# A scheduled trunk of sparse attention, short convolution and SwiGLU: when memory counts as free in the order, and new durations for small operations

## The chip, the core and the metric

The kernel runs on one core of a Trainium2 chip. The core has a matrix engine (PE, whose weight loads are shown apart as PEld), a vector engine (DVE), a scalar engine (ACT), GpSimd (POOL) and the sync engine (SP), from which nearly all DMAs of this kernel are issued. Each engine works off its own queue in order. The metric is the time of one execution on the device in microseconds.

## What is computed

Two decoder layers on 1024 tokens of width 1024, in float32. The first layer mixes tokens by sparse attention: an indexer scores all earlier keys, the best 256 of each query are kept, and attention runs over those. The second mixes by a gated convolution of width 3. Each is followed by a SwiGLU FFN of width 2816, and shift, scale and gate of every norm come from a conditioning vector.

```python
def reference(x, c, positions, ada_w, ada_b, ...):
    c_act = jax.nn.silu(c)
    for i in range(DEPTH):
        mod = c_act @ ada_w[i] + ada_b[i]
        sh1, sc1, g1, sh2, sc2, g2 = [m[:, None, :] for m in jnp.split(mod, 6, axis=-1)]
        h = _rmsnorm(x, norm1_g[i]) * (1.0 + sc1) + sh1
        if i % N_MIXERS == 0:
            y = _dsa_mixer(h, positions, ...)
        else:
            y = _short_conv_mixer(h, ...)
        x = x + g1 * y
        h = _rmsnorm(x, norm2_g[i]) * (1.0 + sc2) + sh2
        x = x + g2 * _swiglu(h, ffn_w_gate[i], ffn_w_up[i], ffn_w_down[i])
    return x
```

## The kernel before

The program is written in two steps. The classes `Attention` and `Tail` record operations with the tiles that they read and write; `Plan` then puts them in order, at build time, and emits them engine by engine. On the chip nothing is decided any more: each engine runs its queue as emitted and waits on semaphores where data or memory aren't ready.

`Plan.drain` is a list scheduler. It holds for each engine the time at which it is free (`self.free`), takes from each engine the recorded operation that could start first, breaks ties by a priority (`pri`, then the order of recording), and places the earliest of all. How long an operation takes is told by `Plan.cost`, in microseconds, from its engine, its name and its free size; `LATENCY` and `SLACK` are added between engines, and a DMA ends after a fixed 1.6 and its bytes at a set rate. A copy recorded by `Plan.copy` may go to ACT or to DVE, whichever is free earlier by these figures. So a price in `cost` never makes anything faster or slower by itself. It only moves operations in the queues.

Memory is handled in pools (`Pool`). Each pool has a gate: no tile of it is given out, in the plan, before `gate.ready`. When a pool is opened (`Plan.open`) this is set to the smallest free time of all engines. What the chip does is apart from that: a pool that lies where another lay waits on the real last use of the tiles there (`reuse_waits="tile"`).

The order of pools stands at the end of `trunk_kernel`. The projections and the selection use `h` and `pj`; attention uses `kp` (the keys, tile `karena`), `at` (rows of the softmax and other small things), the PSUM pool `pa` (banks `ps_L` and `ps_o`), and on the right side `keep`, `sel` and `op` (the attention's output, `ohi` and `olo`). When all operations of `kp`, `at` and `pa` are placed, the pools of the tail are opened in their place: the PSUM pool `pg`, and `x2` (the residual, tile `xr`), `u` and `h2` as `f.first`. When `keep`, `sel` and `op` are done, `t2` and `s2` follow as `f.second`.

Around the first of these changes the following is recorded, all with one priority and so in this sequence: `Attention.attended` makes the eight output tiles of the second half (`out_tile`: a weight load of 512 KB into `raw`, two splits of it into a high and a low half, `whi` on ACT and `wlo` on DVE, 48 matmuls, and an addition into `xr`). After the first of them it starts the tail's first norm of the other half (`norm_first`): eight squares on ACT from `xr` to `u`, sums on DVE, a transposition on PE into `ps_g`, a root, and the operands `h`. A raw tile has two buffers and the split halves four each, so the splits of the third tile wait for matmuls of the first. The sixteen loads of `xr` (`xr<-xs` in the trace) come from DRAM, the half for the output tiles and the half for the norm.

From there on the products of the FFN and the convolution run (`Pair` and `down_pairs`, a Strassen form with seven products for eight), with side steps of the conditioning between them (`adaw` loads, `adacc` on DVE).

All instructions carry line 272, that of the helper that emits them, so the profile is read by tile names.

Of the kernel before, what the change touches and what calls it, by code (L numbers as in the profile page):

```python
# [14 lines left out]
AF = mybir.ActivationFunctionType  # L15
ALU = mybir.AluOpType
AX = mybir.AxisListType
PSUM = bass.MemoryType.PSUM
# [32 lines left out]
class Store:  # L51


    def __init__(self, space):
        self.space, self.real, self.parts = space, None, {}
        self.alloc = None
        self.ring, self.late, self.begun, self.todo, self.last = None, False, False, 0, 0.0
# [49 lines left out]
class Op:  # L107
# [3 lines left out]
    def __init__(self, eng, cost, emit, pri, lat=0.0):  # L111
        self.eng, self.cost, self.emit, self.pri, self.lat = eng, cost, emit, pri, lat
        self.left, self.ready, self.users, self.end, self.stores = 0, 0.0, [], None, ()
        self.late, self.other, self.form = 0.0, None, None
        self.needs, self.parked = [], False


class Pool:


    def __init__(self, plan, name, side=None, space=None, bufs=1, **rings):
        self.depth = rings
        self.plan, self.name, self.side, self.space, self.bufs = plan, name, side, space, bufs
        self.gate = Op(None, 0.0, lambda: None, 0)
        self.gate.left = 1
        self.rings, self.pending = {}, 0

    class Ring:
        def __init__(self, plan, bufs):
# [56 lines left out]
class Plan:  # L186
# [48 lines left out]
    def cost(self, eng, fn, out, ins, kw):  # L235

        n = out.free
        if fn == "dma_start":
            if eng == "gpsimd":
                return 0.85, 1.6  # L240
            inside = len(ins) == 1 and all(r.store.alloc is not None for r in ins + [out])
            return {"sync": 0.65 if inside else 0.475, "scalar": 0.1}[eng], 1.6
        if eng == "tensor":
            if fn == "transpose":
                return 0.107, 0.0
            if ins[1].dtype in (F32R, BF16):
                return max(n, 64) * 17 / 38400.0, 0.0
            return max(n * 4, 512) / (4800.0 if HD in (ins[0].free, ins[0].shape[0]) else
                                      2400.0), 0.0
        psum = any(r.store.space == PSUM for r in ins + [out])  # L250
        m = max([n] + [r.free for r in ins])
        aps = sum(r.free == 1 for r in ins)
        if eng == "scalar":
            return 0.03 + 0.95e-3 * n + (0.09 if "accum_out" in kw else 0.0) + 0.1 * aps, 0.0
        if eng == "vector":
            if fn == "memset":
                return 0.02 + 1.04e-3 * (n if n > P else 0), 0.0
            if fn in ("tensor_scalar", "tensor_copy") and not psum and "accum_out" not in kw:
                return (0.08 if fn == "tensor_copy" else 0.13) + 0.52e-3 * m, 0.0
            if fn == "tensor_scalar" and "accum_out" in kw:  # L260
                return 0.14 + 1.04e-3 * m, 0.0
            return 0.07 + 1.04e-3 * m + (0.05 * aps if m > 64 else 0.0), 0.0
        if fn in ("memset", "affine_select"):
            return 0.05 + 1.4e-3 * n, 0.0
        a, w = (0.28, 1.95e-3) if fn == "tensor_tensor" else (0.43, 1.3e-3)
        return a + w * (n - 1), 0.0
# [34 lines left out]
    def record(self, eng, fn, args, kw, other=None):  # L301
        vals = list(args) + list(kw.values())
        outs = [kw["out"] if "out" in kw else args[0]]
        if "accum_out" in kw:
            outs.append(kw["accum_out"])
        refs = [v for v in vals if isinstance(v, Ref)]
        ins = [v for v in refs if not any(v is o for o in outs)]
        emit = self.emitter(eng, fn, args, kw)
        shaped = outs[0] if isinstance(outs[0], Ref) else refs[0]
        cost, lat = self.cost(eng, fn, shaped, ins, kw)  # L310
        self.count += 1
        pri = (self.count if self.pri is None else self.pri, self.count)
        op = Op(eng, cost, emit, pri, lat)
        if "accum_out" in kw:
            op.late = 0.13 if eng == "vector" else 0.1
        if other is not None:
            op.other = (other[0], self.cost(*other[:2], shaped, ins, kw)[0],
                        self.emitter(*other, args, kw))
        if fn == "dma_start":
            op.lat = lat + shaped.free * shaped.shape[0] * 4 / 380e3  # L320
        self.note(op, refs, outs)
        return op
# [58 lines left out]
            u.ready = max(u.ready, self.after(op, u))  # L381
            self.settle(u)

    def open(self, pool, stack):
        kw = {}
        if pool.space is not None:
            kw["space"] = pool.space
        if pool.side is not None:
            kw["side"] = pool.side
        pool.handle = stack.enter_context(  # L390
            self.tc.tile_pool(name=pool.name, bufs=pool.bufs, reuse_waits="tile", **kw))
        pool.gate.left = 0
        pool.gate.ready = min(self.free.values())
        self.settle(pool.gate)
        return pool

# [84 lines left out]
    def drain(self, *pools):  # L481

        held = []
        while any(p.pending for p in pools) if pools else True:
            best, again = None, False
            for e in self.ENGINES:
                got = self.next(e)
                if got is None:
                    continue
                op = got[3][-1]  # L490
                if op.other is not None and e != op.eng and self.sooner(op, got[0]):
                    held.append((e, op))
                    self.drop(*got[2:])
                    again = True
                    break
                if best is None or got[0] < best[0]:
                    best = got
            if again:
                continue
            for e, op in held:  # L500
                if op.end is None:
                    at = max(op.ready, best[0] if best else 0.0)
                    heapq.heappush(self.soon[e], (at, op.pri, op))
            held = []
            if best is None:
                assert not any(p.pending for p in pools), \
                    "nothing can be issued: " + str([(p.name, p.pending) for p in pools])
                return
            t, e, heap, v = best
            op = v[-1]  # L510
            self.drop(heap, v)
            self.place(op, t)
            if e != op.eng:
                op.eng, op.cost, op.emit = op.other
            op.emit()
            cost = op.cost
            if e == "tensor":
                cost = cost * self.clock(t, cost) + self.CHANGE.get((self.form, op.form), 0.0)
                self.form = op.form
            self.free[e] = end = t + cost  # L520
            if op.lat:
                self.dma = max(self.dma, end) + (op.lat - 1.6)
                end = self.dma + 1.6 + (op.lat - 1.6) * 380e3 * self.TRAIL
                if e == "sync":
                    self.free[e] = max(self.free[e], self.dma - 2.5)
            for st in op.stores:
                if st.alloc is not None:
                    st.pool.pending -= 1
            self.finish(op, end)
            for st in op.stores:  # L530
                st.todo -= 1
                st.last = max(st.last, end if op.lat else end + 0.25)
                if st.todo == 0 and st.ring is not None:
                    st.ring.back(st.last)

# [305 lines left out]
def trunk_kernel(tc, x, c, positions, ada_w, ada_b, norm1_g, norm2_g, attn_w_in, attn_q_norm_g,  # L841
                 attn_k_norm_g, idx_k_ln_g, idx_k_ln_b, attn_w_out, conv_w_in, conv_w,
                 conv_w_out, ffn_w_gate, ffn_w_up, ffn_w_down, rope_c, out):
    plan = Plan(tc.nc, tc)
    with ExitStack() as ctx:
        ctx.enter_context(tc.manual_schedule())
        tk = Trunk(plan)
# [4 lines left out]
        a = Attention(tk, attn_w_in[0], attn_w_out[0], ada_w, xspill)  # L852
# [5 lines left out]
        f = Tail(tk, ada_w, xspill)  # L858
        a.attended(f)
        f.run(ffn_w_gate, ffn_w_up, ffn_w_down, conv_w_in[0], conv_w_out[0], out)  # L860
        right, proj, left = (ctx.enter_context(ExitStack()) for _ in range(3))
# [8 lines left out]
        plan.drain(a.kp, a.at, tk.pa)  # L870
        left.close()
        for p in (tk.pg, *f.first):
            plan.open(p, left)
        plan.drain(a.keep, a.sel, a.op)
        right.close()
        for p in f.second:
            plan.open(p, left)
        plan.drain()


# [1094 lines left out]
```

## Time and profile before

| | us |
|---|---|
| median of 3 runs | 2287.06 (2284.31 to 2287.76) |
| the profiled execution, its time | 2284.62 |
| its span, first to last instruction | 2282.7 |
| PE busy | 2204.1 |
| DVE busy | 1908.3 |
| ACT busy | 1136.6 |

The difference of 1.9 us between time and span lies around the instructions. The mean granted clock of PE was 0.983 of full. Durations of neighbouring instructions on one engine overlap in the profile: the pace is read from the starts of instructions that follow one another, or from a row of several, less one duration. The text tells times from the start of the span; a name such as `whi<-raw` gives the tile written and the tile read.

### The profile page before, as it was taken

How to read it: one execution, taken by the hardware profiler on the slowest of the kernel's cores; microseconds unless marked ns; L12 is line 12 of the kernel's file. 1: busy time of each engine (PE TensorE's matmuls, PEld its weight loads, DVE VectorE, ACT ScalarE, POOL GpSimd, SP SyncE). 2: the span in 40 equal slices, each digit the busy share in tenths (PEclk: the TensorE clock that was granted, in tenths of full speed). 3: DMA queues.
4: the chain of work that ended last, by engine and by line, in shares of the span. 5: the costliest groups of instructions: out<-in, count | busy, mean ns of one | idle time of the engine just before them, and what ended most of it. 6: DMA issues, size and time to landing. Idle time of an engine off the chain costs nothing.

```text
span 2282.7 us, 32575 instructions
## 1 busy us (share of the span) xinstructions
PE 2204.1 (97%) x11435; PEld 1781.5 (78%) x11435; DVE 1908.3 (84%) x3839; ACT 1136.6 (50%) x2152; POOL 4.8 (0%) x19
## 2 busy tenths in 40 slices
PE   4999989999999999999999999999999999999999
PEld 3757866876798878888888778788888888888887
DVE  7899998898589998887788999786898877767974
ACT  4587889857655323333445552224453333334444
POOL 0000000000000000000000000000000000000000
PEclk7999989999999999999999999999999999999999
DMA  9313333542244665544982354424446432339824
GB/s 321 108 47 87 97 104 89 163 147 91 97 140 139 216 215 169 160 147 151 379 306 101 103 165 139 125 79 157 120 125 194 152 120 88 125 128 387 291 89 138
DMA packets 332317, 353.72 MB, mean 155 GB/s; under 512 B 19289, under 2 KB 216954, under 8 KB 332154
## 3 DMA queue, kind: packets, MB, share of 16 engines
q1 hardware_dynamic: 331944, 351.52, 47.6%
q8 instruction: 89, 1.46, 0.3%
q14 instruction: 74, 0.61, 0.1%
q10 hardware_dynamic: 210, 0.14, 0.0%
HBM read 278.97 MB, written 68.94 MB: 152 GB/s over the span
## 4 chain that ended last, share of the span: by engine, by line
PE 71%; DVE 15%; DMA 4%; ACT 2%; issue 2%; SPq 0%; ACTq 0%; DVEq 0%
PE ps_g L272 41%; PE ps_mm L272 28%; DVE u L272 2%; DVE wlo L272 2%; DVE s L272 2%; PE ps_o L272 2%; PE ps_L L272 1%; DVE sc L272 1%; DVE adacc L272 1%; DVE v L272 1%; DMA adaw<-in_ada_w_dram 1%; DVE karena L272 1%; DVE p L272 1%; ACT p L272 1%; DVE cv L272 1%
## 5 line engine op out<-in xcount | busy, mean ns | idle before, releaser
L272 ACT CAST whi<-raw 128x512 fp32r<-128x512 f32 (+1 forms) x312 | 191.8, 619 | 381.0 <-PE ps_g L272 165.9
L272 PE MATMUL ps_g<-t,whi 128*128 128x512 f32 x1184 | 368.8, 393 | 2.4 <-ACT whi L272 2.3
L272 ACT CAST whi<-s 128x512 fp32r<-128x512 f32 x276 | 171.3, 621 | 328.8 <-PE ps_g L272 140.9
L272 PE MATMUL ps_g<-h,whi 128*128 128x512 f32 x1056 | 326.0, 390 | 0.0
L272 DVE TENSOR_TENSOR wlo<-raw,whi 128x512 fp32r<-128x512 f32 (+1 forms) x314 | 214.5, 684 | 76.5 <-ACT whi L272 76.2
L272 PEld LDWEIGHTS ps_g<-t,whi 128*128 128x128 f32 x1184 | 223.7, 190 | 50.8 <-ACT whi L272 4.6
L272 PE MATMUL ps_g<-t,wlo 128*128 128x512 f32 x592 | 233.2, 395 | 4.8 <-DVE wlo L272 4.6
L272 PEld LDWEIGHTS ps_g<-h,whi 128*128 128x128 f32 x1056 | 197.7, 188 | 40.8
L272 PE MATMUL ps_g<-h,wlo 128*128 128x512 f32 x528 | 205.8, 390 | 2.1 <-DVE wlo L272 2.0
L272 DVE TENSOR_TENSOR wlo<-s,whi 128x512 fp32r<-128x512 f32 x276 | 188.0, 684 | 20.9 <-ACT whi L272 19.8
L272 PE MATMUL ps_mm<-t,whi 128*128 128x512 f32 x608 | 188.1, 390 | 0.2
L272 PE MATMUL ps_g<-ph,whi 128*128 128x512 f32 x572 | 179.3, 389 | 0.0
L272 PEld LDWEIGHTS ps_g<-t,wlo 128*128 128x128 f32 x592 | 112.5, 190 | 30.9 <-DVE wlo L272 7.4
L272 PEld LDWEIGHTS ps_mm<-t,whi 128*128 128x128 f32 x608 | 114.4, 188 | 25.2 <-ACT whi L272 0.9
L272 PEld LDWEIGHTS ps_g<-ph,whi 128*128 128x128 f32 x572 | 107.4, 188 | 22.2
L272 DVE TENSOR_TENSOR u<-u 128x512 f32<-128x512 f32 x170 | 114.2, 684 | 7.4 <-ACT u L272 6.2
L272 ACT ACTIVATE junk<-sc,bs 128x896 bf16<-128x896 f32 (+3 forms) x124 | 109.7, 884 | 18.7 <-DVE bs L272 8.7
L272 PE MATMUL ps_mm<-t,wlo 128*128 128x512 f32 x304 | 118.7, 391 | 0.0
L272 PEld LDWEIGHTS ps_g<-h,wlo 128*128 128x128 f32 x528 | 99.1, 188 | 23.5 <-DVE wlo L272 3.0
L272 DVE SCALAR_TENSOR_TENSOR adacc<-adaw,cact,adacc 128x512 f32<-128x512 f32 x140 | 104.2, 745 | 12.6 <-DMA adaw<-in_ada_w_dram 12.2
L272 PE MATMUL ps_g<-ph,wlo 128*128 128x512 f32 x286 | 110.9, 389 | 0.0
L272 PE MATMUL ps_mm<-hhi,whi 128*128 128x512 f32 (+2 forms) x240 | 93.7, 391 | 6.0 <-ACT hhi L272 3.3
(311 smaller groups left out, 4775.2 us busy)
## 6 DMA issues: line engine op xcount, KB each, us to landing
adaw<-in_ada_w_dram SPq DMA_DIRECT2D x160, 256.0 KB, 2.9
ph<-in_ffn_w_down_dram SPq DMA_DIRECT2D x66, 512.0 KB, 6.5
raw<-in_ffn_w_gate_dram SPq DMA_DIRECT2D x54, 512.0 KB, 4.2
raw<-in_ffn_w_up_dram SPq DMA_DIRECT2D x54, 512.0 KB, 4.1
raw<-in_conv_w_in_dram SPq DMA_DIRECT2D x34, 512.0 KB, 4.2
raw<-in_ffn_w_down_dram SPq DMA_DIRECT2D x44, 256.0 KB, 2.7
ph<-in_ffn_w_down_dram SPq DMA_DIRECT2D x44, 256.0 KB, 5.0
raw<-in_attn_w_in_dram SPq DMA_DIRECT2D x18, 512.0 KB, 3.9
```

The lines of the kernel that those rows point to most:

```text
L272: f(*[a.get() if isinstance(a, Ref) else a for a in args], **{k: a.get() if isinstance(a, Ref) else a for k, a in kw.items()})
```

## The change

It has two parts. In the first, a pool remembers the latest end of an operation that used a tile of it (`Pool.last`), `Plan.open` takes the pools whose memory the new one takes over, and the gate is the latest of the smallest free time and their last uses. `pg` follows `pa`; `x2` follows `kp`; `u` and `h2` follow `at`; `t2` and `s2` follow `keep`, `sel` and `op`. The pools opened earlier are as they were. In the second part, `Plan.cost` has other figures for ACT (by where the source lies, and with a term for two functions), for DVE's `tensor_scalar`, scan and reciprocal, and for the common DVE operation, with a least value of 0.09. No operation is added, dropped or given other operands.

```diff
@@ -123,7 +123,7 @@
         self.plan, self.name, self.side, self.space, self.bufs = plan, name, side, space, bufs
         self.gate = Op(None, 0.0, lambda: None, 0)
         self.gate.left = 1
-        self.rings, self.pending = {}, 0
+        self.rings, self.pending, self.last = {}, 0, 0.0
 
     class Ring:
         def __init__(self, plan, bufs):
@@ -251,15 +251,19 @@
         m = max([n] + [r.free for r in ins])
         aps = sum(r.free == 1 for r in ins)
         if eng == "scalar":
-            return 0.03 + 0.95e-3 * n + (0.09 if "accum_out" in kw else 0.0) + 0.1 * aps, 0.0
+            slow = {AF.Silu: 0.06, AF.Square: 0.03}.get(kw.get("func"), 0.0)
+            return ((0.05 if (ins or [out])[0].store.space == PSUM else 0.095) + 0.84e-3 * n + slow +
+                    (0.09 if "accum_out" in kw else 0.0) + 0.1 * aps), 0.0
         if eng == "vector":
             if fn == "memset":
                 return 0.02 + 1.04e-3 * (n if n > P else 0), 0.0
             if fn in ("tensor_scalar", "tensor_copy") and not psum and "accum_out" not in kw:
-                return (0.08 if fn == "tensor_copy" else 0.13) + 0.52e-3 * m, 0.0
+                return 0.08 + (0.52e-3 if fn == "tensor_copy" else 0.59e-3) * m, 0.0
+            if fn in ("tensor_tensor_scan", "reciprocal"):
+                return 0.07 + (2.07e-3 if fn == "tensor_tensor_scan" else 6.25e-3) * m, 0.0
             if fn == "tensor_scalar" and "accum_out" in kw:
                 return 0.14 + 1.04e-3 * m, 0.0
-            return 0.07 + 1.04e-3 * m + (0.05 * aps if m > 64 else 0.0), 0.0
+            return max(0.09, 0.078 + 1.04e-3 * m) + (0.05 * aps if m > 64 else 0.0), 0.0
         if fn in ("memset", "affine_select"):
             return 0.05 + 1.4e-3 * n, 0.0
         a, w = (0.28, 1.95e-3) if fn == "tensor_tensor" else (0.43, 1.3e-3)
@@ -307,7 +311,8 @@
         ins = [v for v in refs if not any(v is o for o in outs)]
         emit = self.emitter(eng, fn, args, kw)
         shaped = outs[0] if isinstance(outs[0], Ref) else refs[0]
-        cost, lat = self.cost(eng, fn, shaped, ins, kw)
+        func = {"func": args[2]} if fn == "activation" else {}
+        cost, lat = self.cost(eng, fn, shaped, ins, {**kw, **func})
         self.count += 1
         pri = (self.count if self.pri is None else self.pri, self.count)
         op = Op(eng, cost, emit, pri, lat)
@@ -381,7 +386,7 @@
             u.ready = max(u.ready, self.after(op, u))
             self.settle(u)
 
-    def open(self, pool, stack):
+    def open(self, pool, stack, *freed):
         kw = {}
         if pool.space is not None:
             kw["space"] = pool.space
@@ -390,7 +395,7 @@
         pool.handle = stack.enter_context(
             self.tc.tile_pool(name=pool.name, bufs=pool.bufs, reuse_waits="tile", **kw))
         pool.gate.left = 0
-        pool.gate.ready = min(self.free.values())
+        pool.gate.ready = max([min(self.free.values())] + [p.last for p in freed])
         self.settle(pool.gate)
         return pool
 
@@ -530,6 +535,8 @@
             for st in op.stores:
                 st.todo -= 1
                 st.last = max(st.last, end if op.lat else end + 0.25)
+                if st.alloc is not None:
+                    st.pool.last = max(st.pool.last, st.last)
                 if st.todo == 0 and st.ring is not None:
                     st.ring.back(st.last)
 
@@ -870,11 +877,11 @@
         plan.drain(a.kp, a.at, tk.pa)
         left.close()
         for p in (tk.pg, *f.first):
-            plan.open(p, left)
+            plan.open(p, left, *(tk.pa,) if p is tk.pg else (a.kp,) if p is f.first[0] else (a.at,))
         plan.drain(a.keep, a.sel, a.op)
         right.close()
         for p in f.second:
-            plan.open(p, left)
+            plan.open(p, left, a.keep, a.sel, a.op)
         plan.drain()
 
 
```

## The prediction

> **What bounds the kernel now.** I read the page first, for the busy shares, then the table of busy time in stretches of 60 us, because this kernel has stages with different limits.
>
> ```profile
> PE 2204.1 (97%) x11435; PEld 1781.5 (78%) x11435; DVE 1908.3 (84%) x3839; ACT 1136.6 (50%) x2152; POOL 4.8 (0%) x19
> ```
>
> ```profile
> 0.00:60.00 60.00, 25.85 (x119) 19.28 (x120) 48.55 (x98) 30.72 (x51) 1.76 (x13) 0.72 0.93 325
> ...
> 300.00:360.00 60.00, 51.22 (x360) 30.72 (x358) 57.01 (x227) 55.73 (x168) 0.00 (x0) 0.83 0.29 80
> ...
> 600.00:660.00 60.00, 55.88 (x491) 54.20 (x488) 36.04 (x61) 28.69 (x50) 0.00 (x0) 0.94 0.38 125
> 660.00:720.00 60.00, 60.00 (x281) 50.08 (x280) 56.90 (x98) 36.48 (x64) 0.00 (x0) 1.00 0.54 161
> ...
> 780.00:840.00 60.00, 59.28 (x261) 47.39 (x260) 57.68 (x98) 18.15 (x30) 0.00 (x0) 1.00 0.67 218
> 840.00:900.00 60.00, 56.88 (x238) 45.83 (x237) 52.22 (x85) 19.77 (x33) 0.00 (x0) 0.94 0.56 175
> ```
>
> The columns are the stretch, its length, then the busy time and count of PE, PEld, DVE, ACT and POOL, the granted clock, the DMA share and GB/s. PE has something to do nearly always, and from 660 us on whole stretches are full of it: there only PE's work sets the pace, and a new order of the others' work is worth nothing. What an order can give lies in the 2282.7 - 2204.1 = 78.6 us in which PE stands idle, and in the clock lost behind those gaps. Of the 78.6, 34.2 (60 - 25.85) lie in the first stretch, where the DMA engines are 0.93 busy. So my question of the trace is where the other 44 us lie and which of them the two edits can reach.
>
> **The first edit: memory that isn't free yet.** The stretch from 600 to 660 holds the change of pools from attention to the tail. I read it on the queues in turn.
>
> ```profile
> SPq L272 <- PE ps_mm L272: 31.3, 1, 31.3
> ```
>
> ```profile
> 606.17 0.66 PE L272 MATMUL ps_mm<-ident,karena 128*128 128x128 f32 x4
> 606.90 9.34 SPq L272 DMA_DIRECT2D xr<-xs  x16
> 616.59 2.66 ACT L272 ACTIVATE u<-xr 128x512 f32<-128x512 f32 x4 [5.02 <-DMA xr<-xs]
> 619.80 2.64 ACT L272 ACTIVATE u<-xr 128x512 f32<-128x512 f32 x4 [0.55 <-DMA xr<-xs]
> 622.35 2.16 ACT L272 CAST whi<-raw 128x512 fp32r<-128x512 f32 x4
> 623.00 0.58 PE L272 MATMUL ps_mm<-ohi,whi 128*128 128x256 f32 x1 [2.35 <-ACT whi L272]
> 625.53 1.11 PE L272 MATMUL ps_g<-ident,u 128*128 128x128 f32 x4 [1.73 <-DVE u L272]
> ```
>
> The tile xr lies where karena lay. SP came to its first load 31.3 us early and stood there until PE had transposed the last of karena (606.17); the 16 loads then went out in 9.34 us. The eight squares of the tail's first norm read the second half of them, which lands last, so the first square starts at 616.59. The four casts of the output weights, whose raw data need nothing of this, stand behind the squares on ACT's queue and start at 622.35; PE, out of weights, waits 2.35 us, and then 1.73 us for the norm's sum. Why they stand in that order is in the code: before, x2's gate is the smallest free time of all engines, and POOL and SP have hardly anything to do, so the planner takes the loads to be early and the squares to be ready well ahead of the casts.
>
> After the change x2's gate is kp's last use. On the chip nothing of the loads moves: they waited for that use anyway. What moves is the planner's idea of when the squares are ready. From 606.9 the planner has sixteen loads at 0.69 us by its own rate; the trace has (619.8 - 606.9) / 16 = 0.81. It will therefore put the squares within one or two us of their true start, and a cast that is ready goes ahead of them. The first four weight units are in use until PE is through with the first two output tiles; the third tile's casts come free as these go, near 616 and 618 by the pace below, among the squares and not behind all eight.
>
> ```profile
> 607.00:620.60 13.60, 13.60 (x129) 13.14 (x127) 3.05 (x6) 4.58 (x9) 0.00 (x0) 1.00 0.85 308
> 620.60:626.00 5.40, 1.32 (x5) 0.98 (x5) 4.84 (x9) 5.11 (x8) 0.00 (x0) 0.70 0.04 6
> 626.00:630.00 4.00, 4.00 (x23) 4.00 (x22) 2.94 (x10) 0.20 (x1) 0.00 (x0) 0.56 0.80 237
> 630.00:663.00 33.00, 33.00 (x276) 32.93 (x275) 25.30 (x39) 16.08 (x27) 0.00 (x0) 1.00 0.33 99
> ```
>
> Undisturbed, PE does 276 instructions in 33.00 us, 0.12 us each. From 620.6 to 630 it did 28 in 9.4 us; at 0.12 they need 3.4. So the place costs **6.0 us**: 4.1 of waiting (2.35 + 1.73) and 1.9 of slow clock (0.70 and 0.56 granted). The price has two ends. If both casts find ACT free, all 6.0 come back; if each of the two casts waits for one square under way (2.66 / 4 = 0.67) and PE feels both, 1.3 stay, 4.7 come back and the slow clock with them or not: without it 2.8. I take **5.5**, the loss less nearly one square, since PE still has the second tile before it when the first cast is due.
>
> On the clock there is a page to weigh. The Trainium skill, "TensorE: Matmul & The Clock Gate", Part 1 (The HAM clock gate), says that the array falls to half speed after an idle window of about 3.4 us. By that rule neither gap, 2.35 or 1.73 us, would slow it, and the place would be worth 4.1 us and no more. The rows with 0.70 and 0.56 speak against so short a reading.
>
> What is late next? PE reaches the tail's first product earlier, so its operands must be there.
>
> ```profile
> 647.40 1.41 DVE L272 SCALAR_TENSOR_TENSOR h<-u,mod,h 128x512 fp32r<-128x512 f32 x2
> ...
> 662.54 0.63 PE L272 MATMUL ps_g<-h,whi 128*128 128x512 f32 x2
> ```
>
> They are done at 648.8, 13.7 us ahead of PE. The change takes 5.5 of that, and may delay the norm: two weight loads of 512 KB can now come between the loads of xr (1.7 us each at 308 GB/s), and casts stand among the squares (4 x 0.54). That is 5.6 at most, so some 2.6 us are left. DVE's and SP's work behind 662 hangs on the last output tile, which PE ends, so it moves along and the gain is kept through the full stretches. The other gates (PSUM pool, u, h2, and the second set behind the last output tile) move nothing: PE is full from 660 to 720, where the second set is first used, and the first u tile waits for xr anyhow. I cost them at nothing; if the early ada loads of the second set go out later, DVE's side steps move, which 60 - 56.90 = 3.1 us of spare DVE time covers.
>
> **The second edit: prices.** No instruction is added, removed or changed, only the durations by which the order is made. How far they were off shows in these rows.
>
> ```profile
> L272 DVE TENSOR_TENSOR_SCAN s<-s 128x1024 f32<-128x1024 f32 x1 | 2.3, 2292 | 0.0
> ...
> L272 DVE RECIPROCAL rst<-rst 128x128 f32<-128x128 f32 x1 | 0.9, 948 | 0.0
> ...
> L272 DVE TENSOR_SCALAR bs<-bs 128x2 int32<-128x2 int32 x90 | 13.7, 164 | 0.9 <-POOL bs L272 0.4
> ```
>
> ```profile
> 306.38 0.48 ACT L272 ACTIVATE p<-p,nm,qsc 128x128 f32<-128x128 f32 x1
> ...
> 306.86 0.48 ACT L272 ACTIVATE p<-p,nm,qsc 128x128 f32<-128x128 f32 x1
> ...
> 593.15 2.01 ACT L272 COPY pf<-ps_mm 128x512 f32<-128x512 f32 x4
> ...
> 833.17 1.28 DVE L272 TENSOR_TENSOR u<-u 128x512 f32<-128x512 f32 x2
> ```
>
> The scan over 1024 was priced at 0.07 + 1.04e-3 x 1024 = 1.13 and is now 2.19, against 2.29 in the trace; over the six scans (4224 elements a row) the planner now sees 4.4 us of DVE time that it had missed. The reciprocal of 128 goes from 0.20 to 0.87 (0.95). The small exponentials follow each other at 0.48; the price goes from 0.44 to 0.49. A copy of 512 out of PSUM follows the last at about (2.01 - 0.58) / 3 = 0.48; 0.52 becomes 0.48. So much is nearer the truth. The common DVE operation over 512 goes the wrong way, from 0.60 to 0.61, where the trace has 1.28 - 0.68 = 0.60. As to time: all of it acts only where PE has gaps that DVE or ACT end, and a shuffle can make gaps as well as close them. Its bounds are the waits that stand there now and as much again below nothing; from 300 to 360 that is 8.8 us of idle PE and (1 - 0.83) x 51.2 = 8.7 of clock, behind it the waits below. I take **0** as the sum of the second edit, since errors of 0.01 to 0.05 us on most groups are small beside what buffers already smooth, and carry +-6 for it.
>
> Sum: 5.5 + 0. The profiled execution took 2284.62 us (span 2282.7), so 2279.1 by its own time; it lies 2.4 under the median of the three runs, 2287.06, for which the forecast is **2281.5 us**.
>
> **The rivals.**
>
> ```profile
> PE ps_L L272 <- DVE mx L272: 8.1, 13, 2.1
> PE ps_g L272 <- DVE wlo L272: 7.2, 6, 3.0
> ```
>
> ```profile
> PE ps_L L272 <- DVE mx L272: 5.1, 6, 2.1
> ```
>
> ```profile
> 848.76 0.80 PE L272 MATMUL ps_g<-t,wlo 128*128 128x512 f32 x1 [3.02 <-DVE wlo L272]
> ```
>
> ```profile
> 837.98 5.53 DMA raw<-in_ffn_w_up_dram
> ...
> 845.49 0.59 DVE adacc L272
> ...
> 848.76 1.65 PE ps_g L272 x3
> ```
>
> First, **the prices pay too**. The waits of PE for mx (8.1 us, 13 times; the row alone below is that of 300 to 400, 5.1 of them) come where ACT's small exponentials and DVE's scans were priced too low. If about half the gaps there and the clock behind them go, that is 6 us more: 2287.1 - 11.5 = 2275.6. For it speaks that DVE and ACT are 57.01 and 55.73 of 60 busy there, so the planner's error hits the bound; against it, that a stage full on both engines has work, not order, as its limit.
>
> Second, **the order at the change of pools stays**: squares are earlier in the record than the casts, so wherever both look ready the squares go first. If the loads land later than planned by 1 to 2 us, or the casts are planned behind the last square, only the wait of 1.73 goes: 2285.4; or one new gap elsewhere gives the gain back: 2287 to 2288.
>
> Third, slower: **DVE becomes the end of the wait in the gate and up products**. From 780 to 850 the chain of waits runs through DVE (57.68 of 60), with a weight load in between, and at 845.49 side steps (adacc) stand ahead of the weights' low half, so that PE waits 3.02 us to 848.76. That gap with its clock, (1 - 0.94) x 60 = 3.6, costs 6.6. The new price makes DVE look 0.01 us slower per operation there, and side steps are placed anew. One more such gap cancels the gain (+1.1); from two on the kernel is slower: 2287.1 - 5.5 + 13.2 = 2294.8. Eleven sets of each FFN offer the place; so far one of 22 fell into it.
>
> **How the numbers follow.** Forecast 0.46, prices pay 0.18, order stays or one new gap 0.20, two new gaps 0.16. About 0.2% (4.6 us) is what a measurement of this kernel can tell from no change. The forecast's gain of 5.5 lies just beyond it: of its 0.46 I count 0.30 as faster, 0.16 as the same. Faster 0.30 + 0.18 = 0.48, same 0.16 + 0.20 = 0.36, slower 0.16. The range goes from 2272 (prices pay, with 4 more) to 2291 (half of the two-gap case inside); about 0.07 lie below and 0.08 above. The forecast's own range, with the +-6, is 2275.5 to 2287.5.
>
> **What would show it.** Right: at the change of pools the first cast of whi lies before or among the squares, SP's loads of xr still start when the last transpose of karena ends, PE has no wait over 1 us between them and the first product on h, and the stretch from 600 to 660 has 59 or more busy and a clock near 1.00. Wrong: the squares still run as two blocks of four ahead of the casts; or the gap has moved to the first product on h; or the gaps of 2 to 3 us from 780 to 1460 have grown in number. The prices show in the stretch from 300 to 360: under 51 us busy or a clock under 0.83 speaks against them.

## The result, and the profile after

The changed kernel takes 2273.68 us (median of 4 runs, 2273.03 to 2276.19); the kernel before took 2285.68 on the same occasions (4 runs). The ratio is 0.9949, with a 95% interval from 0.9932 to 0.9966: half a per cent faster, 12.0 us by the medians. The forecast was 2281.5 with a range from 2272 to 2291, a gain of 5.5 us; the measured gain is more than twice that. The profiled execution took 2273.65, its span is 2271.9.

The page of the kernel after and its stretches of 60 us, those that the prediction showed and three more (360, 420 and 1380):

```profile
PE 2199.9 (97%) x11435; PEld 1779.5 (78%) x11435; DVE 1903.7 (84%) x3828; ACT 1141.0 (50%) x2163; POOL 5.2 (0%) x19
```

```profile
0.00:60.00 60.00, 25.21 (x110) 19.28 (x111) 47.38 (x96) 29.31 (x49) 1.76 (x13) 0.69 0.91 314
...
300.00:360.00 60.00, 55.20 (x390) 33.23 (x391) 59.00 (x238) 57.84 (x175) 0.00 (x0) 0.83 0.31 89
360.00:420.00 60.00, 58.49 (x526) 44.61 (x525) 48.04 (x162) 55.91 (x125) 0.00 (x0) 1.00 0.45 141
420.00:480.00 60.00, 59.66 (x546) 50.47 (x545) 54.07 (x163) 42.89 (x88) 0.00 (x0) 1.00 0.50 150
...
600.00:660.00 60.00, 60.00 (x476) 57.64 (x475) 45.24 (x80) 30.21 (x53) 0.00 (x0) 1.00 0.55 175
660.00:720.00 60.00, 60.00 (x266) 49.73 (x265) 58.76 (x97) 36.45 (x62) 0.00 (x0) 1.00 0.49 146
...
780.00:840.00 60.00, 55.39 (x230) 43.80 (x229) 53.27 (x89) 16.32 (x27) 0.00 (x0) 0.94 0.63 201
840.00:900.00 60.00, 59.59 (x266) 48.69 (x265) 55.85 (x93) 20.77 (x35) 0.00 (x0) 1.00 0.60 186
...
1380.00:1440.00 60.00, 55.79 (x237) 44.67 (x236) 54.16 (x96) 13.81 (x23) 0.00 (x0) 0.97 0.39 119
```

Two of these stretches in the kernel before:

```profile
360.00:420.00 60.00, 57.71 (x522) 43.42 (x520) 48.84 (x162) 53.02 (x122) 0.00 (x0) 1.00 0.47 142
420.00:480.00 60.00, 58.54 (x529) 48.58 (x528) 51.17 (x156) 43.70 (x88) 0.00 (x0) 1.00 0.48 149
```

PE has the same 11435 instructions, and its busy time is nearly the same (2199.9 us for 2204.1). From 600 to 660, the change of pools, PE is full and its clock whole. In attention it is busy 4.0 us more from 300 to 360, at the same clock, and 1.9 us more from 360 to 480. In the tail it stands idle for 4.6 us from 780 to 840, where before 3.1 us were idle one stretch later (840 to 900).

To see where the 10.8 us of span went, three moments of the timeline serve as marks: the first product of attention (`ps_L<-karena,qst`), the end of the last `ps_o` matmul, and the first product on `h` in the tail.

| us | before | after | difference |
|---|---|---|---|
| start to attention's first product | 300.4 | 299.0 | -1.4 |
| from there to the last `ps_o` | 309.9 | 303.7 | -6.2 |
| the change of pools, to the first product on `h` | 52.3 | 45.6 | -6.6 |
| the tail, to the end | 1620.2 | 1623.6 | +3.4 |

Only the third line was forecast as the gain. The first is no larger than what one order of the instructions shows from one execution to the next: the kernels with the changed kernel's order up to there had 299.9 and 300.3. The second is clear of that: attention took 303.7, 302.9 and 304.2 us in the three kernels with this order, and 309.9 to 313.8 in the four with the order of before. ACT's timeline at the change of pools, in the kernel after, with SP's loads and PE's move to the first product:

```profile
599.34 8.37 SPq L276 DMA_DIRECT2D xr<-xs  x16
```

```profile
607.00 0.62 ACT L276 CAST whi<-raw 128x512 fp32r<-128x512 f32 x1 [3.00 <-PE ps_mm L276]
608.43 0.62 ACT L276 CAST whi<-raw 128x512 fp32r<-128x512 f32 x1 [0.82 <-PE ps_mm L276]
608.96 2.19 ACT L276 ACTIVATE u<-xr 128x512 f32<-128x512 f32 x4
611.99 0.63 ACT L276 ACTIVATE u<-xr 128x512 f32<-128x512 f32 x1 [0.83 <-DMA xr<-xs]
612.52 0.60 ACT L276 CAST whi<-raw 128x512 fp32r<-128x512 f32 x1
613.03 1.85 ACT L276 ACTIVATE u<-xr 128x512 f32<-128x512 f32 x3
614.78 0.60 ACT L276 CAST whi<-raw 128x512 fp32r<-128x512 f32 x1
```

```profile
648.22 0.28 PE L276 MATMUL ps_mm<-ohi,wlo 128*128 128x256 f32 x1
648.34 0.63 PE L276 MATMUL ps_g<-h,whi 128*128 128x512 f32 x2
```

The first two casts now stand ahead of the squares, each waiting only for PE to free a weight unit; the next two are threaded between the squares. PE goes from the output tiles into the tail's first product without a wait. SP still waits for karena, and its loads start 3.3 us ahead of the end of the last `ps_o` (602.68), much as before (3.4 us, 606.90 for 610.26):

```profile
SPq L276 <- PE ps_mm L276: 28.4, 1, 28.4
```

### The profile page after: what moved, and what is told of

Its sections match the earlier page's. It is cut to its first block, busy times and chain, and to the rows that moved or that the text cites. A ratio compares the mean times of both kernels' runs of the same rounds, so it can differ in the third digit from the quotient of the medians.

```text
span 2271.9 us, 32575 instructions
## 1 busy us (share of the span) xinstructions
PE 2199.9 (97%) x11435; PEld 1779.5 (78%) x11435; DVE 1903.7 (84%) x3828; ACT 1141.0 (50%) x2163; POOL 5.2 (0%) x19
## 4 chain that ended last, share of the span: by engine, by line
PE 78%; DVE 10%; issue 3%; ACT 2%; DMA 1%; POOL 0%; ACTq 0%; DVEq 0%; POOLq 0%
PE ps_g L276 45%; PE ps_mm L276 31%; PE ps_o L276 2%; DVE u L276 2%; DVE wlo L276 1%; PE ps_L L276 1%; DVE s L276 1%; DVE sc L276 1%; DMA adaw<-in_ada_w_dram 1%; DVE p L276 1%; DVE karena L276 1%; DVE adacc L276 1%; ACT p L276 1%; ACT junk L276 1%; ACT pf L276 0%
## 5 line engine op out<-in xcount | busy, mean ns | idle before, releaser
L276 ACT ACTIVATE junk<-sc,bs 128x384 bf16<-128x384 f32 (+3 forms) x124 | 109.9, 887 | 15.8 <-DVE bs L276 7.7
```

Of the source, the lines that this page charges most:

```text
L276: f(*[a.get() if isinstance(a, Ref) else a for a in args], **{k: a.get() if isinstance(a, Ref) else a for k, a in kw.items()})
```

## The experiments

The theory to be tested: the two edits work at their own places, the gates at the change of pools and the prices in attention because they are nearer the truth. The rivals: the prices alone close the gap; or what the prices did is the luck of one order. A median stands with the ratio to the kernel before and its interval.

### The two edits apart

`gates_only` has the old `cost`. `prices_only` keeps the new one, and in `open`:

```diff
-        pool.gate.ready = max([min(self.free.values())] + [p.last for p in freed])
+        pool.gate.ready = min(self.free.values())
```

> The gates as in the change, all prices as before. Theory (the parts work at their own places): the order up to the change of pools is that of before, so the last ps_o matmul ends near 610.3 us as before; the gap at the change of pools goes, so the first product on h starts 6 to 7 us earlier than before, near 656; the tail is ordered by the old prices and keeps that, so the span is near 2276 and the median 6 to 7 us under before. Rival (the gain came from the prices, and the gap closed because they reshuffled ACT's queue): the casts still stand behind the squares, the first product on h stays near 662, and the time is that of before within 1 us.

> The new prices, every gate as before. Theory: up to the change of pools the order is that of the changed kernel (last ps_o matmul near 602.7); there the casts stand behind the squares again and PE loses about 6 us, so the first product on h starts near 655; the tail is ordered by the new prices and gives back some 3 us as in the changed kernel, so the median lies near 2280, about 5 us under before. Rival (the prices alone close the gap): the first product near 648 and the median near 2274.

Measured: `gates_only` 2280.88 us, 0.9975 [0.9966, 0.9985]; `prices_only` 2281.99, 0.9978 [0.9968, 0.9988]. The product of the ratios is 0.9953, that of both together 0.9949: to within the intervals the edits add up. The change of pools takes 45.6 us with the gates alone and 52.4 with the prices alone. Here is ACT with the new prices and the old gates, and PE's waits there:

```profile
608.48 2.66 ACT L276 ACTIVATE u<-xr 128x512 f32<-128x512 f32 x4 [4.32 <-DMA xr<-xs]
612.27 2.62 ACT L276 ACTIVATE u<-xr 128x512 f32<-128x512 f32 x4 [1.14 <-DMA xr<-xs]
614.79 2.16 ACT L276 CAST whi<-raw 128x512 fp32r<-128x512 f32 x4
```

```profile
615.45 0.39 PE L276 MATMUL ps_mm<-ohi,whi 128*128 128x256 f32 x1 [2.22 <-ACT whi L276]
...
617.98 1.12 PE L276 MATMUL ps_g<-ident,u 128*128 128x128 f32 x4 [1.15 <-DVE u L276]
```

The two blocks of four squares ahead of the four casts are back, and with them the gap. The rival that the prices close it falls. Two expectations were missed: with the gates alone the last `ps_o` ended at 615.3, not near 610.3, and the first product on `h` came at 660.9, not near 656, although the order up to there is that of the kernel before. That is a matter of the clock, told in the last section.

### One gate of the five

In `gate_x2_only` all prices are old and only `x2` gets its gate:

```diff
-            plan.open(p, left, *(tk.pa,) if p is tk.pg else (a.kp,) if p is f.first[0] else (a.at,))
+            plan.open(p, left, *((a.kp,) if p is f.first[0] else ()))
...
-            plan.open(p, left, a.keep, a.sel, a.op)
+            plan.open(p, left)
```

> All prices as before, and of the five gates only that of x2 (on kp). Theory (this gate alone closes the gap, the others move nothing on the path): from the last ps_o matmul to the first product on h 45.6 to 45.8 us as with all gates, against 52.3 before, and the median that of the kernel with all gates and old prices, 2281 within 2. Rival (the PSUM pool's gate or that of u and h2 does part of it): 47 or more.

The change of pools took 45.6 us; the median is 2282.22, 0.9972 [0.9960, 0.9983]. This gate alone does it; the other four move nothing that can be measured.

### Where the prices act

`new_then_old` has the change's gates and its prices up to the recording of the tail, the old prices from there; `old_then_new` the reverse. `act_prices` and `dve_prices` have the gates and one engine's new prices.

```diff
         n = out.free
+        if self.old:
+            return self.cost_old(eng, fn, out, ins, kw)
...
+        plan.old = True
         f = Tail(tk, ada_w, xspill)
```

> The change, but whatever is recorded from the output tiles of the second half on (the tail) is priced as before. Theory (the new prices cost some 3 us in the tail, where DVE's common operation over 512 is now priced above the trace's 0.60): the first product on h near 648 as in the changed kernel, and the tail as long as in the kernel before, 1620 us from there to the end, so the span is near 2268.5 and the median near 2270.3. Rival (what the tail gave back is chance of the order): the length of the tail lies anywhere from 1617 to 1626, and the median from 2267 to 2276.

> The change's gates, the old prices up to the output tiles of the second half and the new ones from there on. Theory: the last ps_o matmul near 610.3 as before, the first product on h near 656, the tail some 3 us longer than before (1623 to 1624), so the span is near 2279 and the median near 2282. Rival (the tail's 3 us are chance): a tail anywhere from 1617 to 1626, the median from 2276 to 2285.

> The gates as in the change, ACT's new prices, DVE's prices as before. Theory A (attention gained because the small exponentials and copies of ACT, off by 0.03 to 0.05 us each in hundreds of operations, are now priced right): the last ps_o matmul ends near 603 us as in the changed kernel, and the median lies near 2272. Theory B (it gained because DVE's scans and reciprocal, 5 us that the planner had missed, now count): the last ps_o matmul near 611, the median near 2280.

> The gates as in the change, DVE's new prices, ACT's prices as before. Theory A: the last ps_o matmul near 611, the median near 2281. Theory B: near 603 and near 2273. If both runs come out between, both groups matter; if one of them is slower than the old prices, the order answers to a new price by chance.

Measured: `new_then_old` 2271.52, 0.9934 [0.9921, 0.9946]; `old_then_new` 2283.68, 0.9985 [0.9976, 0.9994]; `act_prices` 2277.87, 0.9960 [0.9948, 0.9973]; `dve_prices` 2275.45, 0.9952 [0.9938, 0.9965]. The last `ps_o` ended at 604.5, 612.4, 610.9 and 604.4. So what the prices gain lies ahead of the tail. By the last `ps_o` it comes with DVE's prices, which was theory B; the medians of the two runs lie between what the two theories expected, and their intervals overlap, so by the time they don't tell ACT's part from DVE's. The tail of `old_then_new` was 1622.0, not the expected 1623 to 1624; that of `new_then_old` was 1621.4, where 1620 was expected. The next runs try theory B.

### Are the prices better, or is it one lucky order?

`scan_price` has the gates and the old prices, but the scan and the reciprocal as in the change. `dve_602` is the changed kernel with one figure nearer to the trace's 0.60:

```diff
-            return max(0.09, 0.078 + 1.04e-3 * m) + (0.05 * aps if m > 64 else 0.0), 0.0
+            return max(0.09, 0.07 + 1.04e-3 * m) + (0.05 * aps if m > 64 else 0.0), 0.0
```

The `jitter` kernels have the gates, and the new or the old prices times a random factor:

```diff
+        if eng in ("vector", "scalar") and fn != "dma_start":
+            cost *= 1.0 + 0.02 * (2.0 * self.rng.random_sample() - 1.0)
```

> The change's gates and the old prices, but the scan and the reciprocal priced as in the change: of the new prices only those that were off by a factor of two and more. Theory (DVE's missed 5 us carry the gain before the change of pools): the last ps_o matmul near 604 us as with all DVE prices, the median near 2274. Rival (the many small ones carry it): the last ps_o matmul from 609 to 615, the median from 2277 to 2282.

> The changed kernel with DVE's common operation at 0.07 + 1.04e-3 a row element instead of 0.078, so 0.602 at 512 as the trace has it, with the least value of 0.09 kept. Theory (the price of 0.61 costs the tail some 3 us): from the first product on h to the end 1619 to 1620 as with the old prices, last ps_o matmul 600 to 605, the median near 2270. Rival (the tail's length is chance within some 3 us): 1617 to 1624.

> The changed kernel, with each DVE and ACT price multiplied by a random factor from 0.98 to 1.02, other for each operation: an order of the same quality, shuffled. Theory (the gain in attention comes of prices that are nearer the truth): last ps_o matmul from 601 to 606, length from the last ps_o matmul to the first product on h 45.6, median from 2270 to 2277. Rival (the gain is the luck of one order): the last ps_o matmul anywhere from 601 to 615, the median from 2270 to 2285.

> The change's gates and the old prices, shuffled in the same way. Theory: last ps_o matmul from 609 to 616, median from 2277 to 2284, so that old and new prices stay apart whatever the shuffle. Rival (luck): the last ps_o matmul anywhere from 601 to 615.

> The change's gates and the old prices, shuffled by up to 2% with other random factors. Theory (old and new prices stay apart whatever the shuffle): last ps_o matmul from 608 to 616, the median from 2275 to 2284. Rival (luck): the last ps_o matmul below 605.

| kernel (all with the gates) | median us | ratio | last `ps_o` | tail |
|---|---|---|---|---|
| gates_only (old prices) | 2280.88 | 0.9975 [0.9966, 0.9985] | 615.3 | 1618.2 |
| jitter_old_1 | 2277.09 | 0.9961 [0.9950, 0.9972] | 609.3 | 1617.2 |
| jitter_old_2 | 2274.53 | 0.9937 [0.9922, 0.9952] | 606.5 | 1621.0 |
| scan_price | 2272.68 | 0.9932 [0.9914, 0.9950] | 610.0 | 1615.3 |
| the change (new prices) | 2273.68 | 0.9949 [0.9932, 0.9966] | 602.7 | 1623.6 |
| jitter_new_1 | 2268.01 | 0.9920 [0.9896, 0.9943] | 600.2 | 1621.5 |
| dve_602 | 2280.40 | 0.9967 [0.9955, 0.9980] | 615.4 | 1622.2 |

Each `ps_o` and tail here is of one profiled execution, and that can be some us from its kernel's median: `dve_602`'s took 2285.02, the slowest of its six, and `jitter_old_1`'s 2274.11, the fastest of its ten. The medians come from four occasions, on which the kernel before took 2285.68 to 2288.01, so kernels are compared by their ratios.

Theory B falls with `scan_price`: the right price of the scan leaves the last `ps_o` at 610.0, and its good median comes from the shortest tail of all, though no scan is in the tail. The theory of nearer prices is not borne out by `dve_602`: 0.008 us nearer to the trace in the commonest DVE price, and the ratio is 0.9967 for 0.9949, with intervals that overlap. In its profiled execution the last `ps_o` is at 615.4, as late as with the old prices. The waits of PE from 360 to 480 show the loss, first in the changed kernel, then in `dve_602`:

```profile
PE ps_mm L276 <- ACT pf L276: 0.9, 2, 0.5
PE ps_L L276 <- DVE mx L276: 0.7, 2, 0.3
```

```profile
PE ps_L L276 <- DVE mx L276: 2.5, 5, 1.1
PE ps_mm L276 <- ACT pf L276: 2.3, 4, 0.7
PE ps_mm L276 <- DVE on L276: 2.2, 4, 0.9
PE ps_mm L276 <- DVE x L276: 0.7, 1, 0.7
```

No operation is missing or added there; many short waits have come in (1.6 us became 7.7). `jitter_new_1`, at 600.2 and 2268.01, came out below what either of its theories had given for the last `ps_o` and the median. A random 2% on the old prices gained as much as the new ones: 0.9937 in `jitter_old_2`, with the last `ps_o` at 606.5, below its expected 608, and the median of 2274.53 just below the expected 2275. So one order differs from the next by up to 15 us ahead of the change of pools (600.2 to 615.4; executions of one order alone differ by up to 5, as the last section shows), whichever prices made it. Whether the new prices are better on the average stays open: three orders from old prices, jittered or not (615.3, 609.3, 606.5), and three from new ones (602.7, 600.2, 615.4) overlap. What the runs do show is that the old prices' own order is a slow one: with the gates it stands at 0.9975 (0.9972 in `gate_x2_only`), and all eight other orders of the part ahead of the tail have a lower ratio, 0.9920 to 0.9967, the two from old prices with a jitter among them. For the slower of the eight the intervals overlap with that of `gates_only`. Almost any change of the prices might have gained something here, which would also explain that ACT's and DVE's each did; the runs don't settle it.

The tail's length, 1615 to 1624, is also a matter of the order in good part: `scan_price` and `gates_only` have the same prices for all that the tail holds but reciprocals, and differ by 2.9 us. The longer tails do come with the new prices: 1621.3 to 1623.6 in the six kernels that price DVE's work there anew (the change, `prices_only` 1621.9, `old_then_new` 1622.0, `dve_prices` 1621.3 and the two in the table), 1615.3 to 1621.4 in those that don't (`new_then_old` is the 1621.4). The price of 0.61 was supposed to be why, and is not: at 0.60 (`dve_602`) the tail is 1622.2. What it is stays open.

`jitter_new_1`, an order that chance made, has the lowest ratio of all, 0.9920 for 0.9949 of the change, though the two intervals overlap.

## Why the prediction was right

**The gate of x2: right in mechanism and place, a little small.** The squares moved behind the ready casts, the loads of `xr` did not move on the chip, and PE's gap went whole. The term was 5.5 out of a loss put at 6.0; the change of pools became 6.6 us shorter. The 0.5 left for a cast that waits for a square was not needed, since the first two casts came ahead of all squares; and the loss was 0.6 larger than the stretch from 620.6 to 630, worked out at 0.12 us an instruction, had shown.

On the clock, the prediction gave the place 4.1 us if the two gaps left it whole. The place gave 6.6, and `prices_only`, where it stands with 3.6 us of waits, took 6.8 longer than the kernels with the gate: gaps of 2.35 and 1.73 us close together cost clock as well (0.70 granted from 620.6 to 626 and 0.56 from there to 630). That reading came from the Trainium skill's "TensorE: Matmul & The Clock Gate", Part 1 (The HAM clock gate), which has the clock fall after an idle window of about 3.4 us; the trace disagrees with it.

**The other gates at nothing: right** (`gate_x2_only`, 45.6 us). **What is late next: right**, the operands on `h` were in time and the first product follows the last output tile at once.

**The second edit at 0 +- 6: the term that was mis-sized.** With the gates already in, the prices took the ratio from 0.9975 to 0.9949, which is 5.9 us of 2286; without the gates they gave 5.3 (2281.99 for 2287.30). That is the edge of the bounds, and by gain the whole change (12.0 us) lies just beyond 5.5 + 6. The step that failed is "errors of 0.01 to 0.05 us on most groups are small beside what buffers already smooth": a shift of 0.008 us in one price took attention in the profiled executions from 303.7 us to 315.3 and PE's idle time in it from 9.0 us to 17.4. The prices are small, but the order that a list scheduler makes of them is not a smooth function of them. The value of 0 took the old order for a middling one; of the nine orders tried it was the slowest by its ratio. That the time stayed within the stated range is owed to the room left for the first rival, that the prices pay too. This gave 2275.6 and came nearest in time, and its sign (55.20 busy from 300 to 360, for 51.22) is there; but its reason, that attention was priced too low, is not shown: `dve_602` has the same reason and little of the gain, and `jitter_old_2` has the gain without the reason.

**The tail keeps the gain: not quite.** It gave back 3.4 us. The third rival expected few new gaps at 6.6 us each. There were more and smaller ones: the waits of PE over 1 us from 780 us to 1740 went from four (8.2 us together) to nine (13.4 us), while those over 2 us went from two to one. This is not shown to be the whole cause: `dve_602` has four such waits (8.5 us) and a tail of 1622.2 all the same. The largest of the kernel after:

```profile
1398.09 1.48 PE L276 MATMUL ps_g<-t,whi 128*128 128x512 f32 x4 [2.40 <-ACT whi L276]
```

So the forecast's direction rests on a step that was shown. The second half of the measured gain came with the new prices, but a jitter of the old ones gave as much, and the prediction had no reason for it in its sum: nothing in these runs tells that half from luck.

## What to carry to other kernels

In a kernel whose queues a planner fills, look for places where an engine stands in front of work that cannot start yet while ready work waits behind it, and ask which false time made the planner do so: the cure of one such time was worth its gap and the clock lost behind it, and in eleven of the twelve kernels that had it the change of pools took 45.6 to 45.8 us (46.7 in `dve_prices`). Don't credit a new set of prices with what one compiled order does; jitter the prices by a per cent or two first, the old ones too, and see how wide the times spread and where the old order stands among them. And where that spread is wider than the gain, picking the best of several orders is itself an optimisation.

## What the runs showed of the hardware

One order can take different times ahead of the change of pools. The kernel before, `gates_only`, `gate_x2_only` and `old_then_new` have the same order of work on PE, DVE and ACT up to there, and the last `ps_o` ended at 610.3, 615.3, 614.5 and 612.4. Stretches of the kernel before, and then of `gates_only`:

```profile
180.00:200.00 20.00, 17.33 (x79) 13.90 (x78) 19.93 (x68) 14.59 (x28) 0.00 (x0) 0.91 0.49 133
300.00:320.00 20.00, 14.15 (x80) 8.44 (x80) 18.39 (x83) 17.31 (x53) 0.00 (x0) 0.63 0.43 124
320.00:340.00 20.00, 18.78 (x140) 11.23 (x136) 19.35 (x80) 19.00 (x61) 0.00 (x0) 0.86 0.30 87
```

```profile
180.00:200.00 20.00, 17.34 (x67) 14.03 (x66) 18.36 (x60) 12.52 (x22) 0.00 (x0) 0.76 0.48 133
300.00:320.00 20.00, 15.99 (x102) 10.60 (x100) 18.40 (x81) 15.99 (x48) 0.00 (x0) 0.75 0.34 93
320.00:340.00 20.00, 17.50 (x104) 10.71 (x102) 17.78 (x76) 17.62 (x53) 0.00 (x0) 0.65 0.41 119
```

In both, PE waits 2.7 us for the same square of the projections near 188 us. In the first the clock over that stretch is 0.91, in the second 0.76, and attention's first product comes 3.3 us later (303.7 for 300.4). The other 1.7 us of the 5.0 come with the lower clock from 320 to 340. The Trainium skill's "TensorE: Matmul & The Clock Gate", Part 1 (The HAM clock gate), says that the window which sets the clock runs free, so that one kernel is caught by it differently from run to run; these rows agree. Near such a wait, then, a single profile does not give the price of the wait to better than some 3 us. In the changed kernel that wait is 1.62 us and the clock from 180 to 200 is 1.00; in `prices_only`, with the same order, it is 1.66 and 0.91.

The other two differ in another way: up to attention's first product they are as the kernel before (300.7 and 300.6 us). DVE's queue holds side steps of the conditioning (`adacc`) that wait for their weights from DRAM (`adaw`). In `old_then_new` such a wait near 440 us is 3.91 us, for 2.68 in the kernel before. In `gate_x2_only` one stands near 510 us where the kernel before has none. Here are that step and PE's next product, in the kernel before and then in `gate_x2_only`:

```profile
508.06 0.74 DVE L272 SCALAR_TENSOR_TENSOR adacc<-adaw,cact,adacc 128x512 f32<-128x512 f32 x1
510.41 1.55 PE L272 MATMUL ps_L<-karena,qst 64*128 64x512 f32 x6 [0.54 <-DVE mx L272]
```

```profile
510.38 0.75 DVE L272 SCALAR_TENSOR_TENSOR adacc<-adaw,cact,adacc 128x512 f32<-128x512 f32 x1 [1.12 <-DMA adaw<-in_ada_w_dram]
512.75 1.89 PE L272 MATMUL ps_L<-karena,qst 64*128 64x512 f32 x6 [2.04 <-DVE mx L272]
```

PE starts that product 2.3 us later, and the clock from 500 to 520 is 0.91, for 1.00 in the kernel before; together that is most of the 4.2 us.
